# Attention's instruction list made in several passes that hold loads back ahead of moves, and one PSUM pool for the whole kernel

## Chip, core and metric

The kernel runs on one core of a Trainium2 chip. The metric is the device time of one execution in microseconds (us). TensorE (PE) multiplies, with its weight loads listed apart (PEld); VectorE (DVE) and ScalarE (ACT) work on elements; GpSimd (POOL) does small copies; SyncE (SP) issues nearly all DMA transfers, one after the other.

## The reference

A trunk of two layers is applied with shared weights to two groups of tokens, 512 and 256 long, of width 1024. Each layer is a mixer, an MLP and a gated input embedding:

```python
for i in range(DEPTH):
    h = rms_norm(x, norm_mix[i])
    x = x + (window_attention(h, ...) if i % 2 == 0 else short_conv(h, ...))
    h = rms_norm(x, norm_mlp[i])
    x = x + square(relu(h @ mlp_w_up[i])) @ mlp_w_down[i]
    gate = sigmoid(rms_norm(x, norm_ple[i]) @ ple_w_gate[i])
    x = x + (p[i] @ ple_w_proj[i]) * gate
return rms_norm(x, final_norm)
```

The attention has 16 query heads and 4 key heads of 64, a window of 128 tokens either way in blocks of 128 queries, a bias by relative position and a sink logit for each head. All is float32.

## The kernel before

Features lie along the partitions and the 768 tokens of both groups along the free axis. Each float32 operand of a product is split into a high and a low part (ACT copies the high one, DVE subtracts for the low one), and a product is three matmuls: high by high, high by low, low by high.

Attention (`mixer_attention`, some 260 of the 1640 us) is not issued in the order in which it is written. Every instruction or small group is an `Op` with its engine, a cost in us, what it must come after and which buffers it uses. `Plan.order` (L538 to 591) makes a list of them: it simulates the five engines and one pipe for the DMA transfers, and always starts the operation that can start first, on each engine the ready one with the longest way to the end (`reach`). The tiles are allotted and the instructions issued in that list's order. A transfer has a `tail`, the time of its bytes at a given rate, and lands when the pipe has carried all that was issued before it. SP has at most eight transfers under way in the plan.

Three kinds of transfers matter here. **Loads** (`fetched`, and `load_part` for x) bring weights from DRAM into a ring of three buffers `wraw`, or x into `xa`, at a planned 400 GB/s; a `wraw` buffer is free when DVE has made the low part of its weights (`prepared`, L661). **Moves** within the chip are planned at a lower rate: `queries` and `keys` write their high part (`qh`) and low part (`ql`) into rows of the other half of the partitions (192 KB each, 215 GB/s), `skew` is a table of the bias written to DRAM, and `load_bias` reads it back shifted (`bias<-skew`, 300 GB/s). **Stores** of projections (`pj`) are the rest. `dma` (L628) makes them all.

A block of attention (`attend`) is: four heads' scores (`S`, L1087 and L1088, each needs both parts of the moved queries and keys), a reduction with the bias on DVE (L1094), the exponential on ACT, scaling, transposes on PE into `pt` (L1130), a split, the product with the values into `O` (L1145), and two additions on DVE. Products for queries, keys and the output projection (L681) fill PE between the blocks. The output projection adds into `xa` (L1198).

PSUM has eight banks. Attention has a pool of its own with tags `mm0`, `mm1` (one bank each), `S` (3), `O` (1) and `PT` (2); it closes at the end of attention, and a second pool of eight opens with tags `A` (4), `C` (2) and `B` (2), which `bank` (L108) and `fresh` (L111) hand out in the order C, A, B, A for the rest of the kernel. The first products behind attention are the rest of the output projection (`project_add`, L132, added to x at L1281), in code order; then follow the MLP (L465, L1494), the embedding, the convolution and a last stage, which has a list of its own by the same `Plan`.

Of the kernel before, what the change touches and what calls it, by code (L numbers as in the profile page):

```python
# [10 lines left out]
F32 = mybir.dt.float32  # L11
# [3 lines left out]
PSUM = bass.MemoryType.PSUM  # L15
DRAM = bass.MemoryType.DRAM

P = 128
# [11 lines left out]
BM, BS, BO, BT, BL = 1, 3, 1, 2, 5  # L30
# [20 lines left out]
def trunk_kernel(ctx: ExitStack, tc: tile.TileContext, a: dict, out: bass.AP):  # L51
# [52 lines left out]


    BANKS = {"A": 4, "C": 2, "B": 2}

    def bank(tag, name):  # L108
        return psum.tile([P, 512], F32, tag=tag, name=name, bufs=BANKS[tag])

    def fresh(name="mm", n=1, tag=None):  # L111

# [61 lines left out]
    class Norm:  # L174


        n = T

        def __init__(self, i, name, places, acc, rstd=None):
            self.i, self.name, self.places, self.rplace = i, name, places, rstd  # L180
            self.xs = [], []
            self.acc = slot(acc, f"acc_{name}", F32)[:, : self.n]
# [288 lines left out]
    class Op:  # L471
        def __init__(self, engine, cost, run, after, behind, tail):
            self.engine, self.cost, self.run, self.tail = engine, cost, run, tail
            self.after, self.behind = after, behind
            self.start = self.reach = None

    class Plan:


        LATE = 6.0  # L480
        LANES = 8
        OWN = {"PE": 0.0, "ACT": 0.13, "DVE": 0.12, "POOL": 0.1, "SP": 0.0}
        OTHER = {"PE": 0.22, "ACT": 0.15, "DVE": 0.14, "POOL": 0.3, "SP": 0.1}

# [4 lines left out]
        def op(self, engine, cost, run, after=(), uses=(), behind=(), lands=None):  # L489
            flat = []  # L490
            for d in after:
                flat.extend(d if isinstance(d, (list, tuple)) else [d])
            o = Op(engine, cost, run, [d for d in flat if d is not None], list(behind), lands)
            for key in uses:
                assert key not in self.closed, key
                self.users.setdefault(key, []).append(o)
                if key in self.opened and self.opened[key] not in o.after:
                    o.behind.append(self.opened[key])
            self.ops.append(o)
            o.bonus = self.bonus if engine == "PE" else 0.0  # L500
            return o
# [9 lines left out]
        def first(self, box, engine, cost, run, after=(), uses=(), lands=None):  # L511

            def start():
                box.t = box.make()
                run()

            behind = [box.ahead.op] if box.ahead is not None and box.ahead.op is not None else []
            box.op = self.op(engine, cost, start, [box.free, *after], [box.key, *uses], behind, lands)
            self.opened[box.key] = box.op
            return box.op  # L520
# [12 lines left out]
        def done(self, d, engine):  # L533
            if d.tail is not None:
                return d.landed
            return d.start + d.cost + (self.OWN if d.engine == engine else self.OTHER)[d.engine]

        def order(self):  # L538
            after = {id(o): 0 for o in self.ops}
            nexts = {id(o): [] for o in self.ops}  # L540
            for o in self.ops:
                for d in o.after + o.behind:
                    nexts[id(d)].append(o)
                after[id(o)] = len(o.after) + len(o.behind)
            known, sorted_ = dict(after), [o for o in self.ops if after[id(o)] == 0]
            for o in sorted_:
                for n in nexts[id(o)]:
                    known[id(n)] -= 1
                    if known[id(n)] == 0:
                        sorted_.append(n)  # L550
            for o in reversed(sorted_):
                tail = o.tail + self.LATE if o.tail is not None else self.OTHER[o.engine]
                o.reach = o.cost + max((n.reach + (tail if o in n.after else 0.0) for n in nexts[id(o)]), default=0.0)
            free = {e: 0.0 for e in self.OWN}
            waiting = {e: [] for e in self.OWN}
            pipe, landings = 0.0, [0.0] * self.LANES

            def offer(o):
                o.ready = max(
                    [self.done(d, o.engine) for d in o.after] + [d.start for d in o.behind], default=0.0  # L560
                )
                waiting[o.engine].append(o)

            for o in self.ops:
                if after[id(o)] == 0:
                    offer(o)
            out = []
            while any(waiting.values()):
                best = None
                for e, os in waiting.items():  # L570
                    if os:
                        t = max(free[e], min(o.ready for o in os), landings[-self.LANES] if e == "SP" else 0.0)
                        o = max((o for o in os if o.ready <= t), key=lambda o: o.reach + o.bonus)
                        if best is None or t < best[0]:
                            best = t, o
                t, o = best
                waiting[o.engine].remove(o)
                o.start = t
                free[o.engine] = t + o.cost
                if o.tail is not None:  # L580
                    pipe = max(pipe, t + o.cost + 1.3) + o.tail
                    o.landed = pipe + 0.3
                    landings.append(o.landed)
                o.seq = len(out)
                out.append(o)
                for n in nexts[id(o)]:
                    after[id(n)] -= 1
                    if after[id(n)] == 0:
                        offer(n)
            assert len(out) == len(self.ops)  # L590
            return out
# [9 lines left out]

    MM = {512: 0.2275, 384: 0.1743, 256: 0.12}

    def mixer_attention():
        nonlocal tmp
        s1 = ExitStack()
        psum = s1.enter_context(tc.tile_pool(name="psA", bufs=1, space=PSUM))
        ap = s1.enter_context(tc.tile_pool(name="attn", bufs=2))
        tmp = s1.enter_context(tc.tile_pool(name="tmpA", bufs=3))
        odd = s1.enter_context(tc.tile_pool(name="odd", bufs=2))  # L610

        KHI, KLO, QS = (0, 1, 4, 8), (2, 3, 5, 9), (6, 7, 14, 15, 10, 11, 12, 13)
        PB = {"mm0": 1, "mm1": 1, "S": BS, "O": BO, "PT": BT}
        W0 = SEQS[0]
        LW = 3 * P + 1
        plan = Plan()
        op, new, first = plan.op, plan.new, plan.first

        def bank(tag, name="mm"):
            return new(tag, PB[tag], lambda: psum.tile([P, 512], F32, tag=tag, name=name, bufs=PB[tag]))  # L620

# [6 lines left out]
        def dma(box, src, n, after=(), uses=(), queue="SP", rate=400e3):  # L628

            def run():  # L630
                d, s = src()
                (nc.sync if queue == "SP" else act).dma_start(d, s)

            lands = n / rate
            if box is not None and box.op is None:
                return first(box, queue, 0.46, run, after, uses, lands)
            return op(queue, 0.46, run, after, uses, lands=lands)

        def fetched(src):
            n = src.shape[1]  # L640
            raw = new("wraw", 3, lambda: wp.tile([P, CH], F32, name="wraw", bufs=3))
            raw.n = n
            raw.landed = [dma(raw, lambda: (raw.t[:, :n], src), P * 4 * n, uses=())]
            return raw

        def pair_tiles():
# [159 lines left out]
        for n, c in enumerate((slice(0, P), slice(P, 512), slice(512, CH))):  # L806
# [8 lines left out]
            n = c.stop - c.start  # L815
# [46 lines left out]
        for m in range(KB):  # L862
            t = new("L", BL, lambda: odd.tile([P, 2 * LW], F32, tag="L", name="L", bufs=BL)[:, :T])
# [30 lines left out]
        for o, n in ((0, W0), (W0, SEQS[1])):  # L894
            ps = bank("S", "ss")
# [6 lines left out]
        v, ln, y = (temp("n", name) for name in ("v", "ln", "y"))  # L902
# [157 lines left out]
        xa = {}  # L1060
# [127 lines left out]
        def load_part(ms):  # L1188
            for m in ms:
                xa[m] = place(m, "xa", F32)  # L1190
                xa[m].ready = [dma(xa[m], lambda m=m: (xa[m].t[:], a["x"][m]), 393216)]

        def output_part(m, w, n, col=0):
            ops = []
# [71 lines left out]
        return [xa[m].t for m in range(KB)], tuple([aos[k].parts()[p][:] for k in range(KB)] for p in range(2))  # L1266

    xa, aos = mixer_attention()
    psum = ctx.enter_context(tc.tile_pool(name="ps", bufs=8, space=PSUM))
    more = ctx.enter_context(tc.tile_pool(name="more", bufs=1))  # L1270
    tmp = ctx.enter_context(tc.tile_pool(name="tmpB", bufs=1))
    pairs = [main.tile([P, 2, T], F32, tag=f"x{j}", name="x") for j in range(KB // 2)]
# [29 lines left out]
    def run(steps, n=None):  # L1302

        for _ in range(len(steps) if n is None else n):
            steps.pop(0)()
# [459 lines left out]
    def last_stage(y1, y2, own, done, w0, norm, full, rest, prs, kept, accs):  # L1765
# [17 lines left out]
        def ps(tag, name):  # L1783
            return new(tag, BANKS[tag], lambda: bank(tag, name))

# [571 lines left out]
    free = [i for i in xs2 if i not in hs + ls] + wide + [xs0[16], ys[6]]  # L2357
# [6 lines left out]
    behind, product, w0 = second_inputs(n1, xs0[24:])  # L2364
    w = [weight(a["w_o0"][2], 4)] * 2
    w2 = weight(a["w_o2"], 2, tag="z")
    for i, m in enumerate(PAIRED):
        if i == 1:
            w += [weight(a["w_o0"][3], 4)] * 2
        ps = both()  # L2370
# [10 lines left out]
    w2, behind = first_chunk(conv_chunk, n3, 1)  # L2381
# [3 lines left out]
    w1, behind = first_chunk(lambda u: up_chunk(1, u), n4, 2)  # L2385
# [95 lines left out]
```

## Time and profile before

| | |
|---|---|
| runs | 1641.3, 1643.02 and 1644.52 us, median 1643.02 |
| the profiled execution | 1642.33 us |
| its span, first to last instruction | 1640.5 us |
| PE busy | 1625.2 us (99%) |
| weight loads | 1574.3 us (96%) |
| DVE, ACT busy | 1390.1 us (85%), 919.8 us (56%) |
| HBM | 123.85 MB read, 9.96 MB written |

In the profile's lines, times count from the span's first instruction. A line of the timeline has start, length, engine, source line, operation, output<-inputs, shapes, count, and in brackets how long the engine was idle before it and what ended that. SPq is SP issuing a transfer: its length is the issuing, not the transfer. A row of the table by stretches has the stretch, its length, the busy time (and instructions) of PE, PEld, DVE, ACT and POOL, PE's granted clock, the DMA share and GB/s.

### The profile page before, as it was taken

What the parts mean: (1) busy time and instruction counts of PE and PEld (TensorE: products, weight loads), DVE (VectorE), ACT (ScalarE), POOL (GpSimd) and SP (SyncE); (2) the same over time, 40 slices, a digit from 0 to 9 for tenths busy, and PEclk for the clock granted to TensorE, in tenths of its full rate; (3) what the DMA queues carried; (4) which work ended last, traced back from release to release, by engine and by line L of the source; (5) the groups of instructions that cost most, each with busy time, mean ns of one, the idle gap of its engine ahead of it and who ended that gap; (6) DMA issues with size and microseconds to landing.
All of it is one profiled execution on the core that took longest, in us unless ns stands there. A gap on an engine that the chain in (4) does not pass through costs nothing.

```text
span 1640.5 us, 24134 instructions
## 1 busy us (share of the span) xinstructions
PE 1625.2 (99%) x9371; PEld 1574.3 (96%) x9371; DVE 1390.1 (85%) x2214; ACT 919.8 (56%) x1454; POOL 12.0 (1%) x60
## 2 busy tenths in 40 slices
PE   9999999999999999999999999999999999999998
PEld 7988889999999999999999999999999999999987
DVE  7578988999899989977878888768989989999686
ACT  7378885755545545545654344555545545655455
POOL 0000000000000000000000000000000000000000
PEclk9999999999999999999999999999999999999999
DMA  8745302212222222222311222211222122222332
GB/s 309 195 130 137 107 26 97 103 65 78 65 77 69 73 67 87 66 95 76 116 62 52 78 78 77 78 52 58 72 69 86 65 70 73 78 66 77 113 100 90
DMA packets 47822, 144.80 MB, mean 88 GB/s; under 512 B 6075, under 2 KB 9531, under 8 KB 47708
## 3 DMA queue, kind: packets, MB, share of 16 engines
q1 hardware_dynamic: 47564, 143.14, 27.3%
q8 instruction: 73, 1.20, 0.3%
q14 instruction: 41, 0.34, 0.1%
q10 hardware_dynamic: 144, 0.13, 0.0%
HBM read 123.85 MB, written 9.96 MB: 82 GB/s over the span
## 4 chain that ended last, share of the span: by engine, by line
PE 93%; DVE 4%; DMA 2%; ACT 1%; issue 0%; DVEq 0%; SPq 0%; ACTq 0%
PE a L465 33%; PE b L465 8%; PE mm L681 8%; PE mm L132 6%; PE p L1494 6%; PE d L465 5%; PE c L465 5%; PE gate L1828 4%; PE B L465 4%; PE C L465 4%; PE gate L132 3%; PE down L1828 2%; PE pt L1130 1%; PE O L1145 1%; PE S L1087 1%; PE S L1088 1%
## 5 line engine op out<-in xcount | busy, mean ns | idle before, releaser
L433 ACT ACTIVATE whi<-sum 128x1024 fp32r<-128x1024 f32 x66 | 70.2, 1063 | 253.5 <-PE a L465 251.8
L465 PE MATMUL a<-xs,whi 128*128 128x384 f32 x608 | 117.7, 334 | 0.0
L465 PEld LDWEIGHTS a<-xs,whi 128*128 128x128 f32 x608 | 106.4, 188 | 0.4 <-DVE t L2257 0.4
L465 PE MATMUL b<-t,zhi 128*128 128x384 f32 x528 | 106.6, 334 | 0.0
L465 PE MATMUL a<-t,whi 128*128 128x384 f32 x528 | 106.6, 334 | 0.0
L465 PE MATMUL a<-t,zhi 128*128 128x384 f32 x528 | 106.6, 334 | 0.0
L1650 DVE TENSOR_TENSOR x<-x,a 128x384 f32<-128x384 f32 x112 | 62.1, 554 | 51.4 <-PE a L465 51.3
L465 PE MATMUL a<-act,whi 128*128 128x384 f32 x448 | 95.6, 334 | 0.0
L465 PEld LDWEIGHTS a<-t,whi 128*128 128x128 f32 x528 | 92.9, 188 | 0.0
L465 PEld LDWEIGHTS b<-t,zhi 128*128 128x128 f32 x528 | 92.9, 188 | 0.0
L465 PEld LDWEIGHTS a<-t,zhi 128*128 128x128 f32 x528 | 92.9, 188 | 0.0
L433 ACT ACTIVATE zhi<-sum 128x1024 fp32r<-128x1024 f32 x66 | 69.8, 1057 | 40.8 <-DVE sum L409 26.1
L444 DVE TENSOR_TENSOR wlo<-wraw,whi 128x1024 fp32r<-128x1024 f32 x72 | 87.7, 1218 | 0.0
L433 ACT ACTIVATE whi<-wraw 128x1024 fp32r<-128x1024 f32 x72 | 75.8, 1052 | 20.1 <-issue 15.6
L444 DVE TENSOR_TENSOR zlo<-sum,zhi 128x1024 fp32r<-128x1024 f32 x66 | 80.3, 1217 | 0.7 <-ACT zhi L433 0.7
L681 PE MATMUL mm<-xs_mix,whi 128*128 128x512 f32 (+1 forms) x320 | 80.8, 339 | 0.0
L444 DVE TENSOR_TENSOR wlo<-sum,whi 128x1024 fp32r<-128x1024 f32 x66 | 80.4, 1219 | 0.0
L465 PEld LDWEIGHTS a<-act,whi 128*128 128x128 f32 x448 | 79.3, 188 | 0.0
L465 PE MATMUL a<-xs,wlo 128*128 128x384 f32 x304 | 64.9, 334 | 0.0
L465 PE MATMUL b<-t,zlo 128*128 128x384 f32 x264 | 60.9, 334 | 0.0
L465 PE MATMUL a<-t,zlo 128*128 128x384 f32 x264 | 60.9, 334 | 0.0
L465 PE MATMUL a<-t,wlo 128*128 128x384 f32 x264 | 60.9, 334 | 0.0
(396 smaller groups left out, 4479.3 us busy)
## 6 DMA issues: line engine op xcount, KB each, us to landing
wraw<-in_up SPq DMA_DIRECT2D x64, 512.0 KB, 3.4
wraw<-in_down SPq DMA_DIRECT2D x64, 512.0 KB, 3.5
wraw<-in_w_in SPq DMA_DIRECT2D x24, 512.0 KB, 3.4
wraw<-in_gate SPq DMA_DIRECT2D x16, 512.0 KB, 3.5
wraw<-in_w_q SPq DMA_DIRECT2D x8, 512.0 KB, 6.2
wraw<-in_w_out SPq DMA_DIRECT2D x8, 512.0 KB, 3.5
x_in<-in_x SPq DMA_DIRECT2D x8, 384.0 KB, 7.2
pj<-L SPq DMA_DIRECT2D x8, 384.0 KB, 5.9
```

What stands on the lines that cost most here:

```text
L132: pe.matmul(t, lhsT=w, rhs=x[:, o:e], start=first and i == 0 and j == 0, stop=last and i == n - 1 and j == 2)
L433: act.activation(hi[:], src, AF.Copy)
L444: dve.tensor_tensor(lo[:], src, hi[:].bitcast(F32), ALU.subtract)
L465: pe.matmul(ps, lhsT=a, rhs=b, start=start and i == 0, stop=i == len(terms) - 1, skip_group_check=True)
L681: pe.matmul(ps.t[:, :n], lhsT=a_, rhs=b_, start=k == 0 and j == 0, stop=k == len(xs) - 1 and j == 2,)
L1087: pe.matmul(S.t[:, :w], lhsT=q, rhs=khh_[g].t[:, kk], start=True, stop=False)
L1088: pe.matmul(S.t[:, :w], lhsT=q, rhs=kll_[g].t[:, kk], start=False, stop=True)
L1130: pe.transpose(pt.t[:, h * P : (h + 1) * P], lg[h // 2].t[:, h % 2, 1 + b * P : 1 + (b + 1) * P], ident[:],)
L1145: pe.matmul(O.t[:], lhsT=vb, rhs=part.t[:], start=b == 0 and i == 0, stop=b == nk - 1 and i == 1)
L1494: pe.matmul(ps[i][o], lhsT=wt[:, c], rhs=xs[f"x{h + 1}{1 + o}"][m][part], start=k == 0 and j == 0, stop=k == KB - 1 and j == 2,)
L1650: dve.tensor_tensor(t[:, o : o + H], t[:, o : o + H], f, op)
L1828: pe.matmul(ps.t[:, o : o + n], lhsT=a_, rhs=b_, start=begin and i == 0 and j == 0, stop=end and i == len(terms) - 1 and j == 2,)
```

## The change

- `order` makes the list eight times (`PASSES`). The first pass knows no starts. Each later one knows when the pass before started every operation, and how late each could have started without putting off a PE operation (`latest`). The eighth list is used.
- A transfer has a `kind`: `bulk` for loads, `move` for transfers in `dma` with a rate under 400 GB/s, none for the rest. From the second pass on, a load that is SP's next is held while a move is planned to start from 1 us ago up to the load's `tail` plus 1 us ahead, unless the load's latest start is less than 1 us after that move.
- In the model, the first move behind a load that is still in the pipe puts the pipe and that load's landing off by another 1.2 times the load's `tail`.
- One pool holds the PSUM tags of attention for the whole kernel. `A` becomes a round of three `S` banks and the `O` bank, `C` the two `PT` banks, `B` the banks `mm0` and `mm1`.

No instruction on any engine and no transfer is added or removed by the code. The core of the diff:

```diff
     BANKS = {"A": 4, "C": 2, "B": 2}
+    RINGS = {"A": ("S", "S", "S", "O"), "C": ("PT", "PT"), "B": ("mm0", "mm1")}
+    PB = {"mm0": 1, "mm1": 1, "S": BS, "O": BO, "PT": BT}
+    turns = {tag: 0 for tag in RINGS}
 
     def bank(tag, name):
-        return psum.tile([P, 512], F32, tag=tag, name=name, bufs=BANKS[tag])
+        own = RINGS[tag][turns[tag] % BANKS[tag]]
+        turns[tag] += 1
+        return psum.tile([P, 512], F32, tag=own, name=name, bufs=PB[own])
...
+        PASSES, GUARD, AHEAD, MIXED = 8, 1.0, 1.0, 1.2
...
+            for _ in range(self.PASSES):
+                out = self.placed(dict(after), nexts, plans)
+                plans = {id(o): o.start for o in out}
+                end = max(o.start + o.cost for o in out if o.engine == "PE")
+                if best is None or end < best[0] - 1e-9 or len(passes) == self.PASSES - 1:
+                    best = end, out, dict(plans), {id(o): (o.ready, o.landed) for o in out if o.tail is not None}
+                passes.append(end)
+                plans.update(self.latest(out, nexts))
...
+        def latest(self, out, nexts):
+            late = {}
+            for o in reversed(out):
+                lag = o.tail + 2.1 if o.tail is not None else self.OTHER[o.engine]
+                t = min(
+                    (late[id(n)] - (o.cost + lag if o in n.after else 0.0) for n in nexts[id(o)]), default=1e9
+                )
+                late[id(o)] = min(t, o.start) if o.engine == "PE" else t
+            return {("late", k): v for k, v in late.items()}
...
+            moves = [o for o in self.ops if o.kind == "move"] if plans else []
...
                         o = max((o for o in os if o.ready <= t), key=lambda o: o.reach + o.bonus)
+                        while moves and o.kind == "bulk":
+                            soon = [
+                                plans[id(m)]
+                                for m in moves
+                                if id(m) not in gone and t - 1.0 < plans[id(m)] < t + o.tail + self.AHEAD
+                            ]
+                            if not soon or min(soon) + self.GUARD > plans["late", id(o)]:
+                                break
+                            o.ready = max(t, min(soon)) + 0.05
+                            t = max(free[e], min(o.ready for o in os), landings[-self.LANES])
+                            o = max((o for o in os if o.ready <= t), key=lambda o: o.reach + o.bonus)
...
                 if o.tail is not None:
+                    if o.kind == "move" and last is not None and pipe > t + o.cost + 1.3:
+                        pipe += self.MIXED * last.tail
+                        last.landed += self.MIXED * last.tail
+                        last = None
+                    elif o.kind == "bulk":
+                        last = o
                     pipe = max(pipe, t + o.cost + 1.3) + o.tail
...
+    psum = ctx.enter_context(tc.tile_pool(name="ps", bufs=1, space=PSUM))
...
-        psum = s1.enter_context(tc.tile_pool(name="psA", bufs=1, space=PSUM))
...
+            d.kind = "move" if rate < 400e3 else None
...
+            raw.landed[0].kind = "bulk"
...
+                xa[m].ready[0].kind = "bulk"
...
-    psum = ctx.enter_context(tc.tile_pool(name="ps", bufs=8, space=PSUM))
```

More of the change, by code (lines that the diff above doesn't have):

```diff
@@ L473, in __init__ @@
             self.engine, self.cost, self.run, self.tail = engine, cost, run, tail
-            self.after, self.behind = after, behind
+            self.after, self.behind, self.kind = after, behind, None
             self.start = self.reach = None
@@ L550, in order, with rank @@
                         sorted_.append(n)
+            best = None
+            plans, passes = None, []
+            self.rank(sorted_, nexts)
+            for _ in range(self.PASSES):
+                out = self.placed(dict(after), nexts, plans)
+                plans = {id(o): o.start for o in out}
+                end = max(o.start + o.cost for o in out if o.engine == "PE")
+                print("PASS", round(end, 2))
+                if best is None or end < best[0] - 1e-9 or len(passes) == self.PASSES - 1:
+                    best = end, out, dict(plans), {id(o): (o.ready, o.landed) for o in out if o.tail is not None}
+                passes.append(end)
+                plans.update(self.latest(out, nexts))
+            for o in best[1]:
+                o.start = best[2][id(o)]
+                if o.tail is not None:
+                    o.ready, o.landed = best[3][id(o)]
+            for i, o in enumerate(best[1]):
+                o.seq = i
+            return best[1]
+        def latest(self, out, nexts):
[7 more added lines that the diff above has]
+            return {("late", k): v for k, v in late.items()}
+        def rank(self, sorted_, nexts):
             for o in reversed(sorted_):
@@ L553, in order, with placed @@
                 o.reach = o.cost + max((n.reach + (tail if o in n.after else 0.0) for n in nexts[id(o)]), default=0.0)
+        def placed(self, after, nexts, plans):
             free = {e: 0.0 for e in self.OWN}
@@ L567, in order @@
             out = []
+            moves = [o for o in self.ops if o.kind == "move"] if plans else []
+            last = None
+            gone = set()
             while any(waiting.values()):
@@ L578, in order @@
                 o.start = t
+                gone.add(id(o))
                 free[o.engine] = t + o.cost
                 if o.tail is not None:
+                    if o.kind == "move" and last is not None and pipe > t + o.cost + 1.3:
+                        pipe += self.MIXED * last.tail
+                        last.landed += self.MIXED * last.tail
+                        last = None
+                    elif o.kind == "bulk":
+                        last = o
                     pipe = max(pipe, t + o.cost + 1.3) + o.tail
@@ L583, in order @@
                     landings.append(o.landed)
-                o.seq = len(out)
                 out.append(o)
@@ L612, in mixer_attention @@
         KHI, KLO, QS = (0, 1, 4, 8), (2, 3, 5, 9), (6, 7, 14, 15, 10, 11, 12, 13)
-        PB = {"mm0": 1, "mm1": 1, "S": BS, "O": BO, "PT": BT}
         W0 = SEQS[0]
@@ L635, in dma @@
             if box is not None and box.op is None:
-                return first(box, queue, 0.46, run, after, uses, lands)
-            return op(queue, 0.46, run, after, uses, lands=lands)
+                d = first(box, queue, 0.46, run, after, uses, lands)
+            else:
+                d = op(queue, 0.46, run, after, uses, lands=lands)
+            d.kind = "move" if rate < 400e3 else None
+            return d
         def fetched(src):
```

## The prediction, before the result

> **What bounds the kernel now.** I read the table by stretches first, since it says in which stage TensorE (PE) is ever idle; its columns are the length of the stretch, then the busy time of PE, weight loads (PEld), DVE, ACT and POOL, PE's granted clock, the DMA share and GB/s.
>
> ```profile
> 20.00:100.00 80.00, 80.00 (x506) 71.83 (x506) 47.06 (x87) 38.76 (x71) 1.63 (x7) 1.00 0.68 190
> 100.00:240.00 140.00, 135.48 (x830) 117.74 (x829) 127.85 (x361) 121.39 (x306) 9.38 (x41) 1.00 0.40 108
> 240.00:262.00 22.00, 21.33 (x123) 17.90 (x122) 14.78 (x25) 10.89 (x19) 0.00 (x0) 1.00 0.32 101
> 262.00:300.00 38.00, 37.52 (x205) 35.76 (x204) 35.18 (x52) 28.56 (x41) 0.00 (x0) 1.00 0.31 108
> 300.00:1600.00 1300.00, 1299.62 (x7447) 1287.54 (x7446) 1126.46 (x1617) 683.01 (x966) 0.33 (x6) 1.00 0.23 75
> ```
>
> Attention ends near 262 us. Behind it PE is idle 0.48 us up to 300 and 0.38 us in the next 1300, so a microsecond won in attention reaches the end whole. The change touches nothing of the stages behind attention but the names of their PSUM banks. The idle time that the change can reach is therefore that between 20 and 300 us, 0.00 + 4.52 + 0.67 + 0.48 = 5.67 us. The list of PE's waits in this stretch names it (who waits, for whom, total, times, longest):
>
> ```profile
> PE S L1087 <- DMA q<-ql: 4.3, 3, 1.8
> PE mm L132 <- DVE xa L1198: 0.6, 1, 0.6
> PE p L1494 <- DVE zlo L444: 0.5, 1, 0.5
> PE pt L1130 <- ACT L L1117: 0.2, 1, 0.2
> ```
>
> Three waits of a score matmul for a move of queries make three quarters. In the timeline they and the fourth wait have these sizes:
>
> ```profile
> 155.75 0.36 PE L1087 MATMUL S<-kk,q 128*128 128x256 f32 x1 [1.80 <-DMA q<-ql]
> ...
> 166.71 0.36 PE L1087 MATMUL S<-kk,q 128*128 128x256 f32 x1 [1.49 <-DMA q<-ql]
> ...
> 206.43 0.39 PE L1087 MATMUL S<-kk,q 128*128 128x256 f32 x1 [0.98 <-DMA q<-ql]
> ...
> 261.70 0.59 PE L132 MATMUL mm<-aos,whi 128*128 128x384 f32 x2 [0.60 <-DVE xa L1198]
> ```
>
> Why the moves are late is seen in the timeline of SP, which issues all transfers in one order:
>
> ```profile
> 94.64 1.19 SPq L632 DMA_DIRECT2D q<-ql  x2
> ...
> 146.56 1.10 SPq L632 DMA_DIRECT2D q<-qh  x2
> 147.76 0.53 SPq L632 DMA_DIRECT2D wraw<-in_w_o  x1
> 148.39 1.10 SPq L632 DMA_DIRECT2D q<-ql  x2
> 149.58 1.24 SPq L632 DMA_DIRECT2D xa<-in_x  x2
> 150.91 9.17 SPq L632 DMA_DIRECT2D bias<-skew  x8
> 160.18 1.11 SPq L632 DMA_DIRECT2D q<-qh  x2
> 161.38 0.53 SPq L632 DMA_DIRECT2D wraw<-in_w_o  x1
> 162.01 1.10 SPq L632 DMA_DIRECT2D q<-ql  x2
> ...
> 200.28 0.54 SPq L632 DMA_DIRECT2D wraw<-in_w_o  x1
> 200.91 1.10 SPq L632 DMA_DIRECT2D q<-ql  x2
> ```
>
> Ahead of each late pair q<-ql stands a 512 KB load of w_o. DVE's order puts it there: the low part of the weights, which frees the load's buffer, comes just before the low part of the queries.
>
> ```profile
> 145.83 1.23 DVE L661 TENSOR_TENSOR wlo<-wraw,whi 128x1024 fp32r<-128x1024 f32 x1
> 146.97 0.95 DVE L716 TENSOR_TENSOR ql<-qt,qh 128x768 fp32r<-128x768 f32 x1
> ```
>
> The view of the tile q gives the time from issue to landing: first of the pair at 94.64, which has no load ahead, then of those at 148.39, 162.01 and 200.91.
>
> ```profile
> DMA to landing us min/median/max: 3.3/3.5/3.6
> ```
> ```profile
> DMA to landing us min/median/max: 7.2/7.4/7.6
> ```
> ```profile
> DMA to landing us min/median/max: 4.6/4.6/4.7
> ```
> ```profile
> DMA to landing us min/median/max: 5.4/5.5/5.5
> ```
>
> **The change part by part.** No instruction is added or taken away on any engine, and no transfer. What changes is the order in which attention's list is issued, and which PSUM tag a later tile has.
>
> *Holding loads.* When SP would take a load (weights, or x for the residual), it is held if a move is planned to start within the load's own time plus 1 us (512 KB at the planner's 400 GB/s is 1.31, so 2.31 us), unless the load's latest harmless start is less than 1 us behind that move. At 147.76, 161.38 and 200.28 the pair q<-ql follows 0.63 us later, so the load goes behind it. Two gains: SP issues the pair 0.63 us earlier, and it lands some 3.5 us after issue rather than 7.4, 4.6 and 5.5. The pair's first half then lands earlier by (7.2 - 3.3) + 0.63 = 4.5, (4.6 - 3.3) + 0.63 = 1.9 and (5.4 - 3.3) + 0.63 = 2.7 us. Each is more than the wait that it ends (1.80, 1.49, 0.98), so all three go: 4.27 us.
>
> What the holding costs: at the three places nothing. The w_o loads are fetched far ahead. That of 147.76 is converted here:
>
> ```profile
> 197.27 1.04 ACT L657 ACTIVATE whi<-wraw 128x1024 fp32r<-128x1024 f32 x1
> ```
>
> That cover of 49 us is gone only if a load were held for all of it, and then each microsecond of lateness would count in full. The xa loads are needed later still, by the additions of L1198.
>
> What is late next: with the stalls gone DVE has its 127.85 us of work in about 135.7 us, 94%. The nearest row with such a load and no late move is the stretch before:
>
> ```profile
> 100.00:140.00 40.00, 39.84 (x247) 34.51 (x245) 38.06 (x112) 39.33 (x102) 2.59 (x14) 1.00 0.54 152
> ```
>
> There DVE is busy 95% and ACT 98% of the time, and PE loses 0.16 us in 40. At that rate 140 us lose 0.56 us, which I take off. The bounds are 0 and 4.27 (everything given back to DVE, ACT or another move); I stay near the row, since it is the same loop on the same engines.
>
> *Passes and the dearer model.* The list is made eight times, each from the planned starts of the one before, and the eighth is issued whatever its planned end. A move behind a load is charged 1.2 times the load's time more, so PE's order fills a longer wait. This has no row: its price in time lies between a gain of the rest of the idle (0.2 us at L1130) and the loss in the rival on late loads below. I take 0, as no PE work is added and PE's own total is the same. The last stage uses the same planner, but none of its transfers is called a move, so its order stays.
>
> *One pool.* Attention's pool closes before the second one opens, so the first matmul at L132 waits for the last reader of the old banks, the addition at L1198 just before: 0.60 us. With one pool its first two tiles have tag C, that is the two PT banks, last used by attention's transposes, while the last additions hold mm0 and mm1. The 0.60 us go. Does DVE pass this on? It does: it stands idle before its first addition of the next stage, so that one moves up with PE.
>
> ```profile
> 265.99 1.02 DVE L1281 TENSOR_TENSOR x<-xa,mm 128x384 f32<-128x384 f32 x2 [1.69 <-PE mm L132]
> ```
>
> Bounds: 0 (DVE's chain up to 295, where PE waits 0.48 us for zlo, does not move) and 0.60; I take 0.60. The rings hold as many banks as before (4, 2, 2), so nothing else waits for one.
>
> **Sum:** 4.27 - 0.56 + 0.60 = 4.31 us. The profiled execution took 1642.33 us, with a span of 1640.5 and 1.8 around it; it would come to 1638.0. The median of the runs is 1643.02, 0.7 above the profiled one, so the forecast is 1643.02 - 4.31 = **1638.7 us**. About 0.2% (3.3 us) is what a measurement of this kernel can tell from no change; the gain is just above it.
>
> **The rivals.**
>
> *Only the first stall goes.* SP is blocked from 150.91 to 160.08 by eight bias moves, and the high part of the next queries waits behind them:
>
> ```profile
> 157.71 0.83 ACT L713 ACTIVATE qh<-qt 128x768 fp32r<-128x768 f32 x1
> ```
>
> It is ready at 158.54 and issued at 160.18. If bias moves, themselves moves and never held, stand in the way at the second and third place in another form, 1.49 + 0.98 stay and the time is 1643.02 - 1.80 - 0.60 = 1640.6. For it: 9.17 us of SP. Against: the xa loads of 768 KB ahead of these bias moves are held as well.
>
> *The change does not do what it says.* If the latest harmless starts come out early, no load is held, or the reordered list has as much waiting elsewhere. Only the pool's 0.60 is left: 1642.4. Against it stand the 49 us of cover.
>
> *Slower: a load held to its last moment.* Between 30 and 60 us SP's list is nearly all moves, and loads are just in time:
>
> ```profile
> 32.95 1.30 SPq L632 DMA_DIRECT2D wraw<-in_w_v  x1
> ...
> 38.51 3.47 SPq L632 DMA_DIRECT2D bias<-skew  x7
> ...
> 52.08 0.58 SPq L632 DMA_DIRECT2D wraw<-in_p  x1
> ```
> ```profile
> 40.41 0.63 ACT L713 ACTIVATE wvh<-wraw 128x512 fp32r<-128x512 f32 x1 [0.99 <-DMA wraw<-in_w_v]
> ```
>
> A load let go at its last moment stands behind moves. The load at 52.08, behind ten of them, and one at 73.37, alone, took to land:
>
> ```profile
> DMA to landing us min/median/max: 6.4/6.4/6.4
> ```
> ```profile
> DMA to landing us min/median/max: 3.5/3.5/3.5
> ```
>
> That is 2.9 us each. Against it: PE has no idle time at all between 20 and 100, and DVE and ACT are busy 59% and 48%, so there is other work to fill with. It decides from (3.3 + 4.3) / 2.9 = 2.6, three such loads, each stopping PE for the whole of it: 1643.02 - 4.31 + 8.7 = 1647.4.
>
> *More than the stalls.* PE's busy time may hide slack, as matmuls overlap. Weight loads fill 71.83 / 80 = 90% of a stretch in which PE never waits, and 117.74 / 140 = 84% of the main one. If the new list brought the second to the first, that is 140 x 0.057 = 8.0 us, 3.7 beyond the stalls: 1643.02 - 4.31 - 3.7 = 1635.0. Against: the main stretch has transposes and 512-column matmuls that the other has fewer of, and they need fewer weight loads for the time. The Trainium skill (Perfetto Trace Analysis, Identifying the Most-Contended Engine) says to judge TensorE's headroom by the busy share of weight loads, not of matmuls. By that rule this rival would be the likely one; the trace gives it little, since 90% goes with no wait at all.
>
> **How the numbers follow.** Forecast 0.51 (its own range 1637.0 to 1639.7), only the first stall 0.22, no effect 0.10, late loads 0.12, more than the stalls 0.05. Faster by over 0.2% are the first and the last, 0.56; within 0.2% the second and third, 0.32; slower 0.12. The range leaves out late loads and the largest gain, 0.17: from 1636.5 (all of the 5.67 us and 0.9 of hidden slack) to 1645.9 (one late load, 2.9, with all gains given back).
>
> **What would show it.** Right: no wait of S for q<-ql over 0.5 us; no w_o load between q<-qh and q<-ql on SP, and that pair landing in 3 to 4 us; no wait at L132 after the attention's last addition; attention's end near 258 us. Wrong: PE waiting for whi or wlo before 100 us (late loads), S waiting for bias<-skew or for q<-qh (another move in place of this one), or PE idle without a DMA as releaser in the main stretch (DVE or ACT as the bound).

## The result, and the profile after

| | before | after |
|---|---|---|
| median of the runs, same chip | 1642.68 us (6 runs, 1641.3 to 1644.52) | 1636.51 us (6 runs, 1636.08 to 1636.62) |
| ratio of the runs, 95% interval | | 0.9961 (0.9948 to 0.9974) |
| span of the profiled execution | 1640.5 us | 1634.8 us |

The change is faster by 0.39%, 6.2 us between the medians and 5.7 us between the two profiled spans; the forecast was 4.3 us. On another chip the same kernel had a ratio of 0.9953 (0.9941 to 0.9966).

The table by stretches of the changed kernel, with the columns of before (stretch, length, then busy time of PE, PEld, DVE, ACT and POOL, PE's clock, DMA share, GB/s):

```profile
20.00:100.00 80.00, 79.97 (x506) 71.88 (x506) 48.02 (x88) 38.50 (x71) 1.10 (x7) 1.00 0.66 189
100.00:240.00 140.00, 139.49 (x858) 121.34 (x857) 130.44 (x369) 124.82 (x314) 8.95 (x41) 1.00 0.36 108
240.00:262.00 22.00, 21.96 (x130) 19.80 (x129) 15.37 (x22) 9.09 (x12) 0.00 (x0) 1.00 0.44 137
262.00:300.00 38.00, 37.00 (x202) 35.24 (x201) 36.28 (x55) 30.86 (x43) 0.00 (x0) 1.00 0.28 95
```

In the main stretch PE's idle time fell from 4.52 to 0.51 us, and DVE and ACT do 2 and 3% more work in it. Behind attention, between 262 and 300, it rose from 0.48 to 1.00. The list of PE's waits between 20 and 300 us (who waits, for whom, total, times, longest) says why:

```profile
PE p L1560 <- DVE zlo L449: 1.0, 1, 1.0
PE S L1153 <- DVE mn L1160: 0.3, 1, 0.3
PE pt L1196 <- ACT L L1183: 0.2, 1, 0.2
```

Nothing is left of the waits for q<-ql and of the one at the first matmul of the next stage, and the wait for zlo has doubled. SP's timeline shows the loads and moves in their new order, and below it is the time from issue to landing of the low pairs at 147.96, 158.25 and 192.36:

```profile
146.56 1.10 SPq L694 DMA_DIRECT2D q<-qh  x2
147.96 1.10 SPq L694 DMA_DIRECT2D q<-ql  x2
150.55 4.10 SPq L694 DMA_DIRECT2D bias<-skew  x8
156.52 1.11 SPq L694 DMA_DIRECT2D q<-qh  x2
158.25 1.11 SPq L694 DMA_DIRECT2D q<-ql  x2
159.41 0.59 SPq L694 DMA_DIRECT2D wraw<-in_w_o  x1
160.10 0.40 SPq L694 DMA_DIRECT2D xa<-in_x  x1
```
```profile
DMA to landing us min/median/max: 3.1/3.3/3.5
```
```profile
DMA to landing us min/median/max: 2.9/2.9/2.9
```
```profile
DMA to landing us min/median/max: 3.8/4.0/4.1
```

The pairs land in 3 to 4 us where they took 7.4, 4.6 and 5.5. The first w_o load and the xa loads wait until 159 and 160 us, behind the eight bias moves and one more high and low pair. The bias moves, with no loads just ahead of them, keep SP for 4.10 us and not 9.17.

The 5.7 us arise in three places. Attention's last product starts at 256.10 and not at 260.81, 4.71 earlier. The matmul that waits for zlo starts at 290.56 and not at 295.96, 5.40 earlier, so that 0.69 come between the two. The last 0.3 us come in the 1344 us behind; in a second profile of the changed kernel it was 0.1. Two matmuls of the output projection (`mm<-aos,zhi`, 0.17 us each from start to start), which before start at 265.96, behind attention's last product, start at 249.57 after, ahead of it. The rows of after, then of before:

```profile
249.57 0.51 PE L137 MATMUL mm<-aos,zhi 128*128 128x384 f32 x2
...
256.10 0.28 PE L747 MATMUL mm<-aos,wlo 128*128 128x256 f32 x1
256.22 0.52 PE L137 MATMUL mm<-aos,whi 128*128 128x384 f32 x2
...
290.56 0.45 PE L1560 MATMUL p<-x,zlo 128*128 128x384 f32 x1 [1.00 <-DVE zlo L449]
```
```profile
260.81 0.28 PE L681 MATMUL mm<-aos,wlo 128*128 128x256 f32 x1
...
295.96 0.44 PE L1494 MATMUL p<-x,zlo 128*128 128x384 f32 x1 [0.48 <-DVE zlo L444]
```

### The profile page after: what moved, and what is told of

The parts are those of the page before. It is cut to its first block, busy times and chain, and to the rows that moved or that the text cites. A ratio compares the mean times of both kernels' runs of the same rounds, so it can differ in the third digit from the quotient of the medians.

```text
span 1634.8 us, 24125 instructions
## 1 busy us (share of the span) xinstructions
PE 1623.9 (99%) x9371; PEld 1573.5 (96%) x9371; DVE 1390.6 (85%) x2214; ACT 918.9 (56%) x1454; POOL 11.1 (1%) x60
## 4 chain that ended last, share of the span: by engine, by line
PE 96%; DVE 1%; DMA 1%; ACT 1%; issue 0%; SPq 0%; DVEq 0%
PE a L470 34%; PE b L470 8%; PE mm L747 8%; PE mm L137 8%; PE p L1560 6%; PE d L470 5%; PE c L470 5%; PE gate L137 4%; PE gate L1894 4%; PE B L470 4%; PE C L470 4%; PE down L1894 2%; PE O L1211 1%; PE pt L1196 1%; PE S L1153 1%; PE S L1154 1%
```

## The experiments

The theory: a load issued ahead of the low pair makes that pair late, and it is enough to get the load out of its way. The rivals: the new list gains because PE's order fills the wait (passes and dearer charge), or the pool gains more than its wait.

### The pool alone

Before, with the part of the diff that concerns PSUM, and nothing of the planner.

> The kernel before with one PSUM pool, and its list as before. Theory: the wait at the first matmul behind attention (0.60 us, 0.77 from start to start) goes and is kept to the end, some 0.7 us: 1642.0. Rival: the vector engine's chain up to zlo does not move up with it, so the wait there grows from 0.48 to about 1.1 us and nothing is left: 1642.6. The two waits in the profile tell them apart better than the time.

Measured: 1643.0 us, ratio 0.9992 (0.9982 to 1.0001). Its waits of PE between 20 and 300 us, beside the one of 0.2 at pt that before has too:

```profile
PE S L1092 <- DMA q<-ql: 4.3, 3, 1.8
PE p L1498 <- DVE zlo L449: 1.0, 1, 1.0
```

The wait of 0.60 at the first matmul (0.77 from start to start) is gone and the one for zlo has grown by 0.52. On the waits the rival is right: DVE's chain does not come forward as PE does, and most of that gain is handed back 30 us later. Even so something is left in the trace. The two matmuls `mm<-aos,zhi` start at 254.37 here, ahead of attention's last product; they put that product off by 0.17 us and save 0.35 behind it. Counted from the score matmul near 99.2 us, which all the traces have, the matmul that waits for zlo starts 0.53 us earlier than before. By the clock this is not shown: the interval goes from a gain of 0.2% to none.

### The list alone

The changed kernel with two pools, as before.

> The changed kernel with two PSUM pools as before. Theory: the list alone brings 4.7 us (attention's last product moved up by 4.71 us): 1637.3 to 1638.0, with a wait of 0.6 at the first matmul behind attention again. Rival (the pool brings more than its wait, by other bank numbers later on): 1639 or more.

Measured: 1637.26 us, ratio 0.996 (0.9946 to 0.9974), within 0.1 us of the theory's range. The wait of 0.6 is there again; beside the three waits shown, PE has the one of 0.2 at pt between 20 and 300 us:

```profile
PE mm L135 <- DVE xa L1262: 0.6, 1, 0.6
PE p L1558 <- DVE zlo L447: 0.5, 1, 0.5
PE S L1150 <- DVE mn L1157: 0.3, 1, 0.3
```

The matmul that waits for zlo starts 4.83 us earlier than before, counted from the same score matmul; in the changed kernel it is 5.41, so beside the list the pool is worth 0.58 in the trace.

### Four loads moved by hand in the list of before

```diff
-                for o in plan.order():
+                todo = plan.order()
+                for late in [o for o in todo if getattr(o, "w_o", False)]:
+                    sp = [o for o in todo if o.engine == "SP"]
+                    i = sp.index(late)
+                    if i + 1 < len(sp) and getattr(sp[i - 1], "part", None) == 0 and getattr(sp[i + 1], "part", None) == 1:
+                        while getattr(sp[i + 1], "part", None) == 1:
+                            i += 1
+                        todo.remove(late)
+                        todo.insert(todo.index(sp[i]) + 1, late)
+                for o in todo:
                     o.run()
```

> The kernel before with its list, but for four loads of w_o that stood between the high and the low pair of moved queries: each is put behind the low pair. Nothing else is reordered. Theory (the load ahead makes the move late): the three waits of S for q<-ql, 4.3 us, go to under 0.5 in sum, the time falls by 4 to 5: 1638.0 to 1638.7. Rival (the new order of PE's work fills the wait, and the load matters little): at least 3 us of the waits stay: 1641.5 to 1642.7.

Measured: 1637.09 us, ratio 0.9958 (0.9943 to 0.9973); the waits are as the theory had them, and the time is 0.9 us below its range (the kernel before had a median of 1643.98 on this chip). Four transfers in another place, with PE's order untouched, give what the whole new list gives: 4.49 us up to the matmul that waits for zlo, against 4.83. Its waits of PE between 20 and 300 us:

```profile
PE mm L132 <- DVE xa L1199: 0.6, 1, 0.6
PE p L1509 <- DVE zlo L444: 0.5, 1, 0.5
PE S L1088 <- DMA q<-ql: 0.3, 1, 0.3
PE pt L1131 <- ACT L L1118: 0.2, 1, 0.2
```

The three waits of 4.3 us are one of 0.3. This is the cleanest of the runs, since it changes nothing else.

### Three loads put back in the list of after

The same kind of edit the other way: in the changed kernel three w_o loads go ahead of the low pair again.

> The changed kernel with three of its w_o loads put back ahead of the low pair of moved queries (at 147.96, 183.82 and 192.36 us); PE's order stays. Theory: S waits for q<-ql again, by 1 to 2 us at two or three places: 1638.5 to 1641. Rival (PE's order covers it): under 0.5 us of such waits, 1636.5 to 1637.

Measured: 1639.25 us, ratio 0.9977 (0.9967 to 0.9987), 2.7 us above the changed kernel and 2.0 above the list alone on the same chip, as the theory had it. SP's timeline, and two waits of S in PE's:

```profile
147.29 0.53 SPq L694 DMA_DIRECT2D wraw<-in_w_o  x1
147.92 1.10 SPq L694 DMA_DIRECT2D q<-ql  x2
...
193.00 0.55 SPq L694 DMA_DIRECT2D wraw<-in_w_o  x1
193.64 1.10 SPq L694 DMA_DIRECT2D q<-ql  x2
```
```profile
154.78 0.35 PE L1154 MATMUL S<-kk,q 128*128 128x256 f32 x1 [1.29 <-DMA bias<-skew]
```
```profile
200.35 0.35 PE L1154 MATMUL S<-kk,q 128*128 128x256 f32 x1 [1.06 <-DVE heads L1228]
```
```profile
DMA to landing us min/median/max: 6.7/6.9/7.1
```
```profile
DMA to landing us min/median/max: 6.6/6.9/7.2
```

The names in the brackets mislead: the matmul reads kk and q, neither the bias nor heads. The two landing lines belong to the low pairs at 147.92 and 193.64: their first halves land at 147.92 + 6.7 = 154.6 and 193.64 + 6.6 = 200.2, less than 0.2 us before the two scores start. The three stalls of before have the same distance: 148.39 + 7.2 = 155.6 and a start at 155.75, and so on. The name is inferred by the profile; the landing time points at the cause. At the third place, 184.91, the load is issued 2 us ahead of the pair, the pair lands in 4.2 us and S does not wait.

### Holding without the dearer charge, and the charge without holding

```diff
-        PASSES, GUARD, AHEAD, MIXED = 8, 1.0, 1.0, 1.2
+        PASSES, GUARD, AHEAD, MIXED = 8, 1.0, 1.0, 0.0    # hold_no_charge
+        PASSES, GUARD, AHEAD, MIXED = 1, 1.0, 1.0, 1.2    # charge_no_hold
```

> The changed kernel without the dearer model (MIXED 0 in place of 1.2): eight passes, loads held, one pool. Theory (the holding is what gains): the same as the changed kernel, 1636 to 1637, no wait of S for q<-ql over 0.5 us. Rival (the dearer charge, which sets PE's order, does part of it): 1638 or more, with waits of S for a move.

> The changed kernel with a single pass, so that no load is ever held, with the dearer model and one pool. Theory: the w_o loads stand ahead of the low pairs again; the dearer charge shifts PE's order by 1.6 us of expected lateness, which covers part: two waits for q<-ql of 0.5 to 2 us in sum, 1638.5 to 1641. Rival (the charge alone does it): 1637.0 or less and no such wait.

Measured: holding alone 1638.18 us, ratio 0.9972 (0.996 to 0.9984), with no wait of S for a move: the time is the rival's, the waits are the theory's. The charge alone 1637.96 us, 0.997 (0.9959 to 0.9982), below the theory's range and above the rival's, with two such waits. These waits, and the landing of its low pairs at 147.62 and 192.55, the two that have a w_o load just ahead:

```profile
PE S L1153 <- DMA q<-ql: 1.2, 2, 1.0
```
```profile
DMA to landing us min/median/max: 7.0/7.2/7.4
```
```profile
DMA to landing us min/median/max: 6.0/6.2/6.4
```

So the rival has a part: the charge alone saves 3.1 of the 4.3 us of waits. These two pairs land as late as before. S waits 1.00 us for the first and not at all for the second, for which PE has other work. But the list that the charge makes also has no load just ahead of the two other low pairs: the one at 159.95 costs S 0.23 us, and the one at 188.09 lands in 2.9 us. So how much comes from expecting the move late, and how much from loads that got out of the way by themselves, was not separated. Either half of the change does most of the job, and they do not add up.

Holding alone came 1.7 us above the changed kernel although its waits in attention are the same, so both were measured again, on one chip.

> The changed kernel once more, on one chip beside the next three. Theory: 1636.0 to 1637.0, a ratio of 0.996 to the kernel before.

> The changed kernel without the dearer model, beside the changed one. Its first run had no wait of S for a move, yet came to 1638.2. Theory (the charge changes nothing that lasts): the same as the changed kernel within 0.5 us. Rival (the charge is worth something outside the three stalls): 1.2 us or more slower again.

Measured: 1636.55 us, ratio 0.9953 (0.9941 to 0.9966), and 1637.56 us, ratio 0.9961 (0.9948 to 0.9975). The medians are 1.0 us apart, between the two expectations, and the intervals overlap. PE's busy time from 100 to 240 us is 139.50 us in both, and up to the matmul that waits for zlo the two traces agree within 0.03 us. What differs comes later. The wait that differs in the traces is for wlo at the gate product near 800 us, 0.2 against 0.9 us, in a stage that neither list touches. What makes it differ stays open.

### The wait that the pool had lengthened

DVE made wlo, needed later, just ahead of zlo. The edit, on the changed kernel:

```diff
             elif i == 7:
-                ws[1].split("second")
+                ws[1].high("second")
...
         w.split("direct")
+        w.low("second")
```

> The changed kernel, and the vector engine makes zlo ahead of wlo behind attention's output projection, where the matrix engine waits 1.00 us for zlo. Theory: that wait falls by the 1.14 us of the wlo that stood ahead, to under 0.1, and 1.0 us are kept to the end: 1635.5. Rival (wlo is then late, or the stage behind is bound by the vector engine): the wait turns up at a later line, 1636.3 to 1636.8.

> The changed kernel with zlo ahead of wlo, beside the changed one. Theory: 0.8 to 1.2 us less than the changed kernel, as its wait of 1.00 us is gone. Rival: the difference is the chip's, and the two agree within 0.4 us.

Measured: 1635.31 us, ratio 0.9954 (0.9937 to 0.9971), near the theory's 1635.5, then beside the changed kernel 1636.01 us, 0.995 (0.9937 to 0.9962). In the trace the wait for zlo is gone, and PE's waits between 20 and 300 us are these two:

```profile
PE S L1153 <- DVE mn L1160: 0.3, 1, 0.3
PE pt L1196 <- ACT L L1183: 0.2, 1, 0.2
```

The profiled span is 1633.8 us, 1.0 below the 1634.8 of the changed kernel on the same chip. The medians there are 0.5 apart and their intervals overlap, so the gain is shown by the trace and not by the clock: 0.5 lies between the two expectations, and the execution profiled here is the fastest of its five. Counted from the score matmul near 99.2 us, the matmul that waited for zlo starts 1.2 us earlier.

### All three places by hand, on the list of before

The four moved loads, one pool, and the swap; no passes, no holding rule, no dearer charge.

> The kernel before with its own list, the four w_o loads put behind the low pairs by hand, one pool, and zlo ahead of wlo: none of the passes, of the holding rule or of the dearer model. Theory (these three places are all that the change gains): as fast as the changed kernel with the swap, 1635.0 to 1636.0. Rival (the passes find more than the four places): at least 1 us slower than that.

Measured: 1635.14 us, ratio 0.9945 (0.9932 to 0.9957), the lowest of all. One wait of PE is left between 20 and 300 us:

```profile
PE pt L1136 <- ACT L L1123: 0.2, 1, 0.2
```

Up to the matmul that waited for zlo its trace agrees with that of the changed kernel with the swap within 0.03 us. The passes find no more than these places.

### Only transfers, on an idle chip

Moves of 192 KB (`q`), w_o loads of 512 KB (`raw`) and x loads of 384 KB (`xa`), in groups, each group waiting for the one before.

> All computation is left out and the output is zeros: only transfers of the sizes in question on an idle chip, group by group, each twice: high pair and low pair of moves; the same with a 512 KB load between; the load alone; three loads; and with two xa loads behind, with the load between the pairs or behind both. If a load ahead costs a move its bytes alone, the low pair lands 1.3 to 1.6 us later behind the load, some 4.7 to 5.2 us from issue in place of 3.3; if loads and moves in one queue slow each other, by 3 us or more, 6 to 7 us from issue. If the 7.2 us in the kernel need the engines' own traffic, the idle chip shows about 5.

SP's timeline of one group with the load between the pairs:

```profile
73.78 0.54 SPq L68 DMA_DIRECT2D raw<-in_w_o  x1
74.41 1.10 SPq L65 DMA_DIRECT2D q<-src  x2
```

From issue to landing, in this order: the low pair without a load (at 67.18), the low pair behind the load, the load between the pairs (at 73.78), a load alone, and three loads in a row.

```profile
DMA to landing us min/median/max: 3.2/3.3/3.4
```
```profile
DMA to landing us min/median/max: 6.5/6.5/6.5
```
```profile
DMA to landing us min/median/max: 6.8/6.8/6.8
```
```profile
DMA to landing us min/median/max: 3.4/3.4/3.4
```
```profile
DMA to landing us min/median/max: 3.7/4.6/5.6
```

With nothing else on the chip the pair behind a load takes 3.2 us longer to land, so the engines' own traffic is not needed. And it is not the load's bytes: three loads in a row, issued 0.4 and 0.5 us apart, land 1.3 and 1.5 us apart (1.3 and 1.7 in the other round), while a load between moves takes 6.8 us in place of 3.4 itself. With two x loads behind, the low pair took 7.2 to 7.8 us with the load between the pairs, and 3.2 to 3.5 with the load behind both: the cure shows on the idle chip as well. Loads and moves in one queue slow each other. Of the first round its first group is left aside: there, 10 us into the run, the pairs took 6.5 to 7.5 us without any load, and why is open.

## Why the prediction was right or wrong

**The cause** was right. The load ahead of the low pair makes it late (shown by moving four loads, and by putting three back), holding it costs no wait, and the pair then lands in 3 to 4 us. All three stalls go. One reading was wrong and changes nothing: only the load at 147.76 has 512 KB, those at 161.38 and 200.28 have 384, so the planner's time for them is 0.98 us and the rule reaches 1.98 us ahead, still past the 0.63 to the pair.

**The size of the stalls** was the step that failed: 4.27 us, read as PE's idle time. PE's gain up to attention's last product is 4.71 us, where the sum has 4.27 - 0.56 = 3.71. Of the 1.00 us between them the idle time explains 0.30: it fell from 4.59 us (5.19 between 20 and 262, less the 0.60 at the pool) to 0.58, that is by 4.01. The other 0.70 was listed as busy time; with the two matmuls that now stand ahead of that product it is 1.05. In the timeline of before:

```profile
153.56 0.40 PE L1145 MATMUL O<-pl,vv 128*128 128x512 f32 x1
```
```profile
247.45 0.39 PE L1145 MATMUL O<-pl,vv 128*128 128x512 f32 x1
247.68 0.39 PE L1145 MATMUL O<-ph,vv 128*128 128x512 f32 x1
```

A matmul of 512 columns is listed as 0.4 us long, but the next one starts 0.23 us after it. Behind the one at 153.56 the next starts at 155.75, 2.19 later: the stall took 1.96 us, of which 1.80 are listed as idle. In the same way the second took 1.65 and the third, behind a transpose whose usual distance is 0.11, 1.15. The three together took 4.76, not 4.27, so 0.49 of the 1.05 are theirs. The new wait below takes 0.16 back, and the rest, some 0.7 us, is spread over the stretch in pieces of under 0.25 us, whose cause no run here shows.

**New small waits**, 0.56: idle time of 0.51 us is left in the main stretch, but only 0.33 of it is new; the rest stood there before, and the sum took it off all the same. From start to start the new wait took 0.49 (0.60 behind a transpose), so the term was near.

**The pool**, 0.60: in the traces it is worth 0.53 alone and 0.58 beside the list, so the size was near, but by luck. The reason given, that DVE passes the gain on, was wrong: from start to start the first wait is 0.77, and 0.52 came back at zlo, by just the mechanism that was named for the bound of 0. The rest comes from the two matmuls that start ahead of attention's last product, which the prediction did not foresee; what puts them there was not settled.

**The dearer charge**, taken as 0: right for the waits in attention and wrong as a reason. Alone it saves 3.1 us of waits; beside the holding there is no such wait left for it to save. Holding alone came out 1.7 and 1.0 us slower, which the traces show behind attention; whether the charge has to do with that stays open.

**The rivals.** That bias moves keep the second stall did not happen. The reason given against it, the xa loads that are held, is not what decides: with the four loads moved by hand the xa loads still stand ahead of the bias moves, these keep SP for 6.45 us, and 0.30 us are left of the second stall. In the trace of before, five of the eight bias moves are issued 0.01 to 0.06 us after an earlier transfer lands: at 154.65, 155.68, 156.50, 157.80 and 159.78, behind the w_o load (154.63), the late pair (155.62 and 156.48) and the xa loads (157.79 and 159.76). By these times SP was waiting for the late transfers themselves, so the first load out of place had a part in the second stall too.

No load came late: PE is idle 0.03 us between 20 and 100.

The largest gain, by the share of weight loads, was forecast at 1635.0, and the median of 1636.51 lies nearer to it than to 1638.7. It had the sign of what was missed, time lost within busy time, but not the size: the share of weight loads did not come to 90%, it is 121.34 of 140 us, 87%, with 0.51 us of idle time. And of the two forms that were said to set the stretches apart only the transposes do, some 200 against 15; matmuls of 512 columns are as dense in both, 2.1 in a microsecond. The Trainium skill's rule (Perfetto Trace Analysis, Identifying the Most-Contended Engine) that matmul busy time is a bad measure is borne out by the 0.70 us above; the weight loads' share did not measure it either, the distance from start to start did.

**The runs.** The profiled execution of before, 1642.33 us, lies low among the 44 runs of that kernel in four sets, 1641.3 to 1646.3 us, while the changed kernel's eleven lie between 1636.1 and 1637.3. The medians are therefore further apart (6.2 and 7.9 us) than the profiled spans. Of the 1.9 us between 6.2 and the forecast, 1.0 comes up to attention's last product, where the step failed, and 0.5 is this difference between medians and spans; the other 0.4 comes behind attention, 0.1 up to zlo and 0.3 after it. What scatters the runs of before, by 2.4 to 4.4 us in a set, was not settled: other kernels with loads ahead of the pairs scatter by about 2 us, but so does the one that holds without the charge.

## What to carry to other kernels

Where moves within the chip and loads share a queue, issue the urgent move first, and look for loads that slip in because a buffer comes free in just that gap: a load that is wanted 50 us later can stop the critical engine now. Measure a stall of PE from start to start, against the usual distance of such matmuls, since idle time leaves out what the last matmul still shows as busy. When a wait is taken away, the next stage's slowest chain must move too, or the gain returns there as another wait. Here DVE's two low parts in the other order took that wait away in the trace, while the clock could not tell it.

## What the runs showed of the hardware

A 512 KB load between moves of 192 KB takes about twice as long to land as alone (6.8 to 7.3 us against 3.2 to 3.4). On the idle chip the high pair lands 2.7 and 2.9 us after its issue at 72.6 and 73.1, the load 6.8 after 73.78 and the low pair 6.5 after 74.41 and 74.92: 896 KB in the 4.5 to 5.3 us behind the high pair, where the pair alone takes some 1.6 us more than the high one and a load in a row 1.3 to 1.7. The load and the pair behind it land within 0.9 us of each other, as if they shared the engines. The Trainium skill (DMA: Bandwidth & Descriptors, Specifications) gives about 358 GB/s as the limit from HBM for one core, which would be an estimated 1.5 us for 512 KB; loads in a row agree, loads among moves do not, and the measurement decides.
